# An encoder layer on one core: a ring of its own for weight sums made by DMA, two plain blocks instead of four, the last rows by halves

## The chip, the core and the metric

The kernel runs on one core of one Trainium2 chip, as a single program. The time is the device time of one execution in microseconds (us). Three executions of the kernel before took 1315.06, 1314.51 and 1313.67 us: median 1314.51 us. The engines are TensorE (PE, which also loads weights: PEld), VectorE (DVE), ScalarE (ACT), GpSimd (POOL) and SyncE (SP, which issues most DMAs). Each engine works through its own list of instructions in order and waits on semaphores for the others.

## What is computed

One encoder layer on x of 512 tokens by 1024 features, in float32:

```python
def swiglu(x, w1, w3, w2):
    return (jax.nn.silu(x @ w1) * (x @ w3)) @ w2
...
# x = x + 1/2 * SwiGLU_1(RMSNorm(x))        "ffn a", D_FF = 2816
# x = x + mix(RMSNorm(x))                   two attention branches, gates, w_out
# x = x + 1/2 * SwiGLU_2(RMSNorm(x))        "ffn b"
# output: RMSNorm(x)
```

Each RMSNorm divides by the root of the mean square of a token's 1024 features and multiplies by a gain. The change leaves the attention in the middle alone.

## The kernel before

**Layout.** x lies transposed in eight tiles x[d] of 128 features by 512 tokens. Every product is made of three fp32r matmuls (mm3, lines 195 to 199): each operand is split into a rounded part H and a remainder L, and H*H, H*L and L*H are added. A weight tile of 128x1024 (512 KB) comes by DMA into a raw buffer; ACT casts it to wh (L180) and DVE makes wl (L181) in prep. The raw tiles lie in rings, in which a new tile takes the oldest buffer once its last reader is done: wr (3 buffers), wa (3) and ws (2). The wh/wl pairs have a ring of 3 and one extra buffer, so a wl is made at most some four weight tiles ahead of PE.

**A feed-forward stage.** The 22 blocks of 128 hidden features run in this order: first some plain blocks, by 512-column matmuls (pair, feat; 48 matmuls a block), then groups of pairs of blocks by a Strassen scheme (strassen), each group followed by the eight output rows of w2 that its blocks feed (blocks). GROUPS gives the bounds: in ffn a four plain blocks, then pairs up to 8, 16 and 22, that is groups of 2, 4 and 3 pairs; in ffn b two plain blocks and groups of 3, 4 and 3 pairs. A pair of blocks is seven products, named A11, S1, S2, A12, S3, S4 and A22, each of 24 matmuls of 256 columns: 168 in all, where two plain blocks take 96 matmuls of 512 columns. The pairs are interleaved: pair i has its products at places 7i, 7i+2, ... 7i+12 (slots).

**Weight sums.** A11, A12 and A22 are quarters of the weights as they are. The raws of S1 and S3 are sums: SP loads A21 (L163), and when it has landed POOL issues a DMA that adds A22 or A11 to it in place (L164). S2 and S4 are made by DVE from raws that are there already (L179): S2 = S1 + A11, S4 = S2 + A12. Before the change S1 and S3 lie in wr, beside A22, the plain tiles and the w2 tiles.

**T, statistics and held blocks.** The right operands of S1, S2, S3 and A22 are four sums of quarters of h (TH, TL), made in 16 steps (t_steps, L275 to L283) that the plain part's loop emits between matmuls: hooks["T"] = (first step n, every). The plain part runs before the factors R of the RMSNorm are known: its PSUM banks (the ring "mm" has four) are held, and its evictions (L394, L398, L379) are emitted at the hook stat_R. stat_r (L328, L329, L336) sums the squares on PE, takes ms on DVE and the power on POOL; stat_R (L344, L346) spreads r over the partitions with PE (rb) and copies it to R with ACT. Each hook's n counts the mm3 groups of the plain part.

**The order.** The order on PE is that of the code. The order on ACT, DVE, POOL and SP is set by a list scheduler at build time, from estimated costs. On the chip each engine keeps that order: an instruction that waits holds everything behind it.

**The end.** ffn b's last rows add to x (L443, L444), its squares go to acc, and the last of the eight rows is done in two halves of 256 tokens: after half 0, tail(0) finishes the norm of these tokens and writes them, while PE works on half 1; tail(1) comes after the last matmul (L488 to L518). In tail, POOL does two of the eight multiplications and DVE six (L498).

Of the kernel before, what the change touches and what calls it, by code (L numbers as in the profile page):

```python
# [11 lines left out]
F32 = mybir.dt.float32  # L12
F32R = mybir.dt.float32r
AF = mybir.ActivationFunctionType
# [1 line left out]
PSUM = bass.MemoryType.PSUM  # L16
DRAM = bass.MemoryType.DRAM

BUFS = {"wr": 3, "wa": 3, "ws": 2, "wh": 3, "whx": 1}
GROUPS = {"a": (4, 8, 16, 22), "b": (2, 8, 16, 22)}  # L20
STEPS = ("A11", "S1", "S2", "A12", "S3", "S4", "A22")
GAP_X = 8
GAP_V = 4
# [3 lines left out]
T = 512  # L27
D = 1024
NK = 8
# [11 lines left out]
G_FFN1, G_MIX, G_FFN2, G_FIN, G_BG = 0, 8, 16, 24, 32  # L41
# [14 lines left out]
class Layer:  # L56
# [78 lines left out]
    def load(self):  # L135
        n = len(self.raws)
        if n == len(self.order):
            return False
        name, key = self.order[n][:2]
        tag, last = "wr", n  # L140
        if name[:2] == "sw":
            f, step = key
            tag = {"A11": "wa", "A12": "wa", "S2": "ws", "S4": "ws"}.get(step, "wr")
            last = self.index.get((name, (f, {"A11": "S2", "S1": "S2", "A12": "S4", "S2": "S4"}.get(step))), n)
        raw = self.ring(tag, n, len(self.tiles), last)
        if raw is None:
            return False
        self.raws.append(raw)
        nc = self.nc
        if name[:2] != "sw":  # L150
            nc.sync.dma_start(raw, self.a[name][key])
            return True
        w = self.a["w13" + name[2]]
        dst = raw.rearrange("p (a c) -> p a c", a=2)

        def part(q):
            i, c = 2 * f + int(q[1]) - 1, 512 * (int(q[2]) - 1)
            return w[i:i + 3:2, :, c:c + 512].rearrange("a p c -> p a c")

        if step[0] == "A":  # L160
            nc.sync.dma_start(dst, part(step))
        elif tag == "wr":
            nc.sync.dma_start(dst, part("A21"))  # L163
            nc.gpsimd.dma_start(dst, part("A22" if step == "S1" else "A11"), accum_op=ALU.add)  # L164
        return True
# [148 lines left out]
    def norm_sq(self, d):  # L314
        nc = self.nc
        if d == 0:
            nc.scalar.activation(self.acc, self.x[d], AF.Square)
        else:
            sq = self.tmp.tile([128, T], F32, tag="sq", name="sq", bufs=2)
            nc.scalar.activation(sq, self.x[d], AF.Square)  # L320
            eng = nc.vector if d >= NK - 2 else nc.gpsimd
            eng.tensor_add(self.acc, self.acc, sq)
# [44 lines left out]
    def ffn_run(self, s, gin, gnext, hooks, out, side, gp):  # L367
        nc = self.nc
        g, t, c, half = [], {}, {}, []
# [96 lines left out]
        lo, n = first, 0  # L466
# [15 lines left out]
            g.clear()  # L482
        if out is None:
            return
        self.blocks("w2" + s, rows[:-1], n)
        d, nf = NK - 1, len(g)
        ws = [self.block("w2" + s, n + d * nf + f) for f in range(nf)]
        halves = []  # L488

        def tail(hf):  # L490
            cs = slice(256 * hf, 256 * hf + 256)
            tiles = range(2 * hf, 2 * hf + 2)
            self.stat_r([self.acc[:, :], halves[hf]], tiles)
            yield
            self.stat_R(tiles)
            for e in range(NK):
                y = self.x[e][:, cs]
                (nc.gpsimd if e in (1, 4) else nc.vector).tensor_mul(y, y, self.R[:, cs])  # L498
                (nc.scalar if hf and e % 2 else nc.sync).dma_start(out[e][:, cs], y)
            yield  # L500

        first = None
        for hf in range(2):
            cs = slice(256 * hf, 256 * hf + 256)
            ps = self.bank()
            for f in range(nf):
                self.mm3(ps[:, 0:256], *ws[f], g[f][0][:, cs], g[f][1][:, cs], f == 0, f == nf - 1)
                if hf and f in (nf // 2, nf - 1):
                    next(first)
            xs = self.x[d][:, cs]  # L510
            add(xs, ps[:, 0:256], self.R[:, cs])
            sq = self.tmp.tile([128, 256], F32, tag="sqh", name="sqh", bufs=2)
            nc.scalar.activation(sq, xs, AF.Square)
            nc.scalar.activation(xs, xs, AF.Copy, scale=self.par[:, gnext + d:gnext + d + 1])
            halves.append(sq)
            first = first or tail(0)
        for _ in tail(1):
            pass  # L518

    def bias_open(self, bp):  # L520
# [220 lines left out]
    def rope(self, grp, i, b):  # L741
# [7 lines left out]
        if grp == 0:  # L749
            nc.scalar.activation(self.vH[:, i, :], b[:, 256:512], AF.Copy, scale=rc)  # L750
            nc.vector.scalar_tensor_tensor(self.vL[:, i, :], b[:, 256:512], rc, f32(self.vH)[:, i, :], op0=ALU.mult, op1=ALU.subtract)
        sq = self.tmp.tile([128, T], F32, tag="sq", name="sqb", bufs=2)
        nc.scalar.activation(sq[:, :w], xk[:, :w], AF.Square)
        ss = self.tmp.tile([128, 4], F32, tag="ss", name="ss")
        nc.vector.tensor_reduce(ss[:, :nh], sq[:, :w].rearrange("p (h d) -> p h d", d=128), axis=mybir.AxisListType.X, op=ALU.add)
# [161 lines left out]
    def layer(self, out):  # L917
# [19 lines left out]
                self.norm_sq(d)  # L937

        with tc.tile_pool(name="bt", bufs=1, side="right") as bp:
            hooks = {8: squares, 22: self.stat_r, 26: self.stat_R, "T": (10, 2)}  # L940
            self.bias_open(bp)
            side = {(0, d): lambda g=d: self.bias_rows(g) for d in range(3)}
            for h in range(8):
                side[(0, 4 + h) if h < 4 else (1, h - 4)] = lambda h=h: self.bias_spread(h)
            self.ffn("a", G_FFN1, G_MIX, hooks, side=side)
        self.mixer()
        self.ffn("b", G_FFN2, G_FIN, {7: self.stat_r, 12: self.stat_R, "T": (1, 1)}, out)
        self.hctx.close()


# [92 lines left out]
```

## Time and profile before

| | before |
|---|---|
| median of three executions | 1314.51 us (1313.67 to 1315.06) |
| the profiled execution | 1316.43 us |
| its span (first to last instruction) | 1314.7 us |
| PE busy in the span | 1284.9 us (98%) |
| DVE busy | 832.8 us (63%) |
| ACT busy | 554.4 us (42%) |
| DMA, mean over the span | 124 GB/s |
| stages: plain part of ffn a, last matmul of ffn b | 5.13 to 55.60, 1301.89 us |

A row of a timeline is: start in us from the span's start, duration, engine, line, operation, output <- input, count, and in brackets how long the engine had been idle before it and who released it. A row of a table of windows gives for a stretch its length, the busy time of the engines with the count of instructions, the clock that PE was granted (1.00 is full), the busy share of the DMA engines and GB/s. The profiled execution is 1.7 us longer than its span and 1.9 us above the median.

### The profile page before, as it was taken

The numbers are of one execution on the slowest core, as the hardware profiler recorded it, in microseconds if no ns is written. First come the engines' busy times: TensorE is split into PE (matmuls) and PEld (weight loads), VectorE is DVE, ScalarE is ACT, GpSimd is POOL, SyncE is SP. The second block draws the span as 40 slices with busy tenths as digits, with TensorE's granted clock in tenths as the row PEclk, the third lists the DMA queues.
The fourth block names the chain that finished last, engine by engine and source line by source line (L and its number), as shares of the span: only waits on it lengthen the run. The fifth ranks groups of instructions, "written<-read, shape, count | busy, mean of one in ns | idle before, by whom it ended". The sixth has DMA issues, their size and how long they took to land.

```text
span 1314.7 us, 18852 instructions
## 1 busy us (share of the span) xinstructions
PE 1284.9 (98%) x7580; PEld 1113.4 (85%) x7580; DVE 832.8 (63%) x1227; ACT 554.4 (42%) x829; POOL 120.7 (9%) x106
## 2 busy tenths in 40 slices
PE   7999999999999999999999999999999999999996
PEld 6897999899789877777887778888879989988985
DVE  7775578568632346554575899654487756765774
ACT  7551345145422244144233465543375415432552
POOL 2101100100200000000022300000211010100103
PEclk9999999999999999999999999999999999999998
DMA  7655866544333333232332311345256456645521
GB/s 246 147 172 152 220 162 175 133 124 131 95 96 96 96 87 92 81 82 66 124 98 80 98 63 48 109 157 167 96 128 171 151 128 163 173 130 144 140 86 64
DMA packets 75863, 163.48 MB, mean 124 GB/s; under 512 B 11760, under 2 KB 18304, under 8 KB 75776
## 3 DMA queue, kind: packets, MB, share of 16 engines
q1 hardware_dynamic: 63984, 138.12, 33.4%
q0 software_dynamic: 11072, 23.61, 10.3%
q8 instruction: 59, 0.97, 0.3%
q10 hardware_dynamic: 720, 0.55, 0.1%
q14 instruction: 28, 0.23, 0.1%
HBM read 155.87 MB, written 10.04 MB: 126 GB/s over the span
## 4 chain that ended last, share of the span: by engine, by line
PE 86%; DVE 5%; ACT 3%; issue 2%; DMA 1%; POOL 1%; SPq 0%; DVEq 0%; ACTq 0%; POOLq 0%
PE mm L197 23%; PE mm L199 23%; PE mm L198 23%; PE Y L199 2%; PE Y L198 2%; PE Y L197 2%; ACT P L640 2%; PE S L626 1%; PE X L197 1%; PE X L199 1%; PE X L198 1%; PE Tb L807 1%; PE mm L677 1%; DVE wl L181 1%; DMA wr<-in_w13b 1%
## 5 line engine op out<-in xcount | busy, mean ns | idle before, releaser
L180 ACT CAST wh<-wr 128x1024 fp32r<-128x1024 f32 x195 | 203.8, 1049 | 413.3 <-PE mm L198 287.3
L181 DVE TENSOR_TENSOR wl<-wr,wh 128x1024 fp32r<-128x1024 f32 x195 | 238.3, 1222 | 107.4 <-ACT wh L180 107.0
L197 PE MATMUL mm<-hH,wh 128*128 128x512 f32 (+1 forms) x568 | 212.0, 373 | 5.1 <-ACT wh L931 5.1
L199 PE MATMUL mm<-hH,wl 128*128 128x512 f32 (+1 forms) x568 | 207.6, 365 | 1.2 <-DVE wl L932 0.7
L198 PE MATMUL mm<-hL,wh 128*128 128x512 f32 (+1 forms) x568 | 207.1, 365 | 0.7 <-DVE hL L312 0.6
L198 PE MATMUL mm<-gg,wh 128*128 128x512 f32 (+1 forms) x358 | 139.8, 391 | 1.5 <-DVE gg L389 1.5
L197 PE MATMUL mm<-gg,wh 128*128 128x512 f32 (+1 forms) x358 | 140.2, 392 | 0.2
L199 PE MATMUL mm<-gg,wl 128*128 128x512 f32 (+1 forms) x358 | 139.7, 390 | 0.0
L199 PE MATMUL mm<-TH,wl 128*128 128x256 f32 x456 | 128.1, 281 | 4.0 <-DVE wl L181 4.0
L197 PEld LDWEIGHTS mm<-hH,wh 128*128 128x128 f32 x568 | 107.8, 190 | 25.8 <-ACT wh L931 5.1
L198 PE MATMUL mm<-TL,wh 128*128 128x256 f32 x456 | 127.7, 280 | 0.0
L197 PE MATMUL mm<-TH,wh 128*128 128x256 f32 x456 | 127.7, 280 | 0.0
L199 PEld LDWEIGHTS mm<-hH,wl 128*128 128x128 f32 x568 | 107.4, 189 | 19.9 <-DVE wl L932 1.1
L198 PEld LDWEIGHTS mm<-hL,wh 128*128 128x128 f32 x568 | 107.6, 190 | 17.8 <-DVE hL L312 1.7
L199 PEld LDWEIGHTS mm<-TH,wl 128*128 128x128 f32 x456 | 86.5, 190 | 4.4 <-DVE wl L181 4.4
L197 PEld LDWEIGHTS mm<-TH,wh 128*128 128x128 f32 x456 | 86.5, 190 | 0.0
L198 PEld LDWEIGHTS mm<-TL,wh 128*128 128x128 f32 x456 | 86.4, 189 | 0.0
L198 PEld LDWEIGHTS mm<-gg,wh 128*128 128x128 f32 x358 | 67.4, 188 | 16.9 <-DVE gg L389 2.5
L197 PEld LDWEIGHTS mm<-gg,wh 128*128 128x128 f32 x358 | 67.4, 188 | 16.9 <-ACT gg L388 1.0
L443 DVE TENSOR_TENSOR u<-mm,R 128x512 f32<-128x512 f32 (+1 forms) x49 | 33.3, 679 | 74.1 <-PE mm L199 73.8
L199 PEld LDWEIGHTS mm<-gg,wl 128*128 128x128 f32 x358 | 67.4, 188 | 14.7
L197 PE MATMUL mm<-wh,hH 128*128 128x512 f32 x192 | 77.0, 401 | 0.0
(194 smaller groups left out, 2590.9 us busy)
## 6 DMA issues: line engine op xcount, KB each, us to landing
wr<-in_w13b SPq DMA_DIRECT2D x34, 512.0 KB, 3.7
wr<-in_w13a SPq DMA_DIRECT2D x33, 512.0 KB, 3.8
wr<-in_waq SPq DMA_DIRECT2D x24, 512.0 KB, 3.6
wr<-in_w2a SPq DMA_DIRECT2D x22, 512.0 KB, 3.6
wr<-in_w2b SPq DMA_DIRECT2D x22, 512.0 KB, 3.5
wa<-in_w13b SPq DMA_DIRECT2D x20, 512.0 KB, 3.9
wr<-in_w13b POOLq DMA_DIRECT2D x20, 512.0 KB, 5.8
wa<-in_w13a SPq DMA_DIRECT2D x18, 512.0 KB, 4.1
```

The lines of the kernel that those rows point to most:

```text
L180: self.nc.scalar.copy(H, raw)
L181: self.nc.vector.tensor_sub(L, raw, f32(H))
L197: mm(out, lH, rH, start=start, stop=False, skip_group_check=more)
L198: mm(out, lH, rL, start=False, stop=False, skip_group_check=more)
L199: mm(out, lL, rH, start=False, stop=stop, skip_group_check=more)
L443: nc.vector.tensor_mul(u, ps, R)
L626: nc.tensor.matmul(*args, start=True, stop=True)
L640: nc.scalar.activation(sl, sl, AF.Exp, bias=SO[:, 0, li, h:h + 1], scale=1.0, accum_out=SO[:, 0, li, 2 + h:3 + h])
L677: nc.tensor.matmul(oc, v, p, start=st, stop=sp)
L807: nc.tensor.transpose(pt[:, 128 * j:128 * j + 128], P[h, j][:, 128 * k:128 * k + 128], self.ident)
```

## The change

Five things change. S1 and S3 get a ring of their own, wt, of two buffers, and wa goes from three to two. ffn a has two plain blocks and one more Strassen pair in its first group (3, 4 and 3 pairs, as in ffn b), and its T steps are emitted at every mm3 group from the 10th on instead of at every second one. The squares share the ring "t". In ffn b stat_R stands at the 15th mm3 group of the plain part instead of the 12th. And at the end the last four rows (d = 4 to 7) go by halves: all four rows for tokens 0 to 255, then all four for the rest, with the norm of half 0 spread over the rows of half 1, all its multiplications on DVE, and the sums into acc of these rows on DVE too.

```diff
--- before.py
+++ after.py
@@ -16,8 +16,8 @@
 PSUM = bass.MemoryType.PSUM
 DRAM = bass.MemoryType.DRAM
 
-BUFS = {"wr": 3, "wa": 3, "ws": 2, "wh": 3, "whx": 1}
-GROUPS = {"a": (4, 8, 16, 22), "b": (2, 8, 16, 22)}
+BUFS = {"wr": 3, "wa": 2, "ws": 2, "wt": 2, "wh": 3, "whx": 1}
+GROUPS = {"a": (2, 8, 16, 22), "b": (2, 8, 16, 22)}
 STEPS = ("A11", "S1", "S2", "A12", "S3", "S4", "A22")
 GAP_X = 8
 GAP_V = 4
@@ -140,7 +140,7 @@
         tag, last = "wr", n
         if name[:2] == "sw":
             f, step = key
-            tag = {"A11": "wa", "A12": "wa", "S2": "ws", "S4": "ws"}.get(step, "wr")
+            tag = {"A11": "wa", "A12": "wa", "S2": "ws", "S4": "ws", "S1": "wt", "S3": "wt"}.get(step, "wr")
             last = self.index.get((name, (f, {"A11": "S2", "S1": "S2", "A12": "S4", "S2": "S4"}.get(step))), n)
         raw = self.ring(tag, n, len(self.tiles), last)
         if raw is None:
@@ -159,7 +159,7 @@
 
         if step[0] == "A":
             nc.sync.dma_start(dst, part(step))
-        elif tag == "wr":
+        elif tag == "wt":
             nc.sync.dma_start(dst, part("A21"))
             nc.gpsimd.dma_start(dst, part("A22" if step == "S1" else "A11"), accum_op=ALU.add)
         return True
@@ -316,7 +316,7 @@
         if d == 0:
             nc.scalar.activation(self.acc, self.x[d], AF.Square)
         else:
-            sq = self.tmp.tile([128, T], F32, tag="sq", name="sq", bufs=2)
+            sq = self.tmp.tile([128, T], F32, tag="t", name="sq")
             nc.scalar.activation(sq, self.x[d], AF.Square)
             eng = nc.vector if d >= NK - 2 else nc.gpsimd
             eng.tensor_add(self.acc, self.acc, sq)
@@ -482,39 +482,43 @@
             g.clear()
         if out is None:
             return
-        self.blocks("w2" + s, rows[:-1], n)
-        d, nf = NK - 1, len(g)
-        ws = [self.block("w2" + s, n + d * nf + f) for f in range(nf)]
-        halves = []
-
-        def tail(hf):
+        nf, half = len(g), NK // 2
+        self.blocks("w2" + s, rows[:half], n)
+        ws = [[self.block("w2" + s, n + d * nf + f) for f in range(nf)] for d in range(half, NK)]
+
+        def norm(hf):
             cs = slice(256 * hf, 256 * hf + 256)
             tiles = range(2 * hf, 2 * hf + 2)
-            self.stat_r([self.acc[:, :], halves[hf]], tiles)
+            self.stat_r([self.acc[:, :], sqs[hf]], tiles)
             yield
             self.stat_R(tiles)
             for e in range(NK):
                 y = self.x[e][:, cs]
-                (nc.gpsimd if e in (1, 4) else nc.vector).tensor_mul(y, y, self.R[:, cs])
+                nc.vector.tensor_mul(y, y, self.R[:, cs])
                 (nc.scalar if hf and e % 2 else nc.sync).dma_start(out[e][:, cs], y)
-            yield
-
-        first = None
+                if e % 3 == 2:
+                    yield
+
+        sqs, first = [], iter(())
         for hf in range(2):
             cs = slice(256 * hf, 256 * hf + 256)
-            ps = self.bank()
-            for f in range(nf):
-                self.mm3(ps[:, 0:256], *ws[f], g[f][0][:, cs], g[f][1][:, cs], f == 0, f == nf - 1)
-                if hf and f in (nf // 2, nf - 1):
-                    next(first)
-            xs = self.x[d][:, cs]
-            add(xs, ps[:, 0:256], self.R[:, cs])
-            sq = self.tmp.tile([128, 256], F32, tag="sqh", name="sqh", bufs=2)
-            nc.scalar.activation(sq, xs, AF.Square)
-            nc.scalar.activation(xs, xs, AF.Copy, scale=self.par[:, gnext + d:gnext + d + 1])
-            halves.append(sq)
-            first = first or tail(0)
-        for _ in tail(1):
+            for d in range(half, NK):
+                ps = self.bank()
+                for f in range(nf):
+                    self.mm3(ps[:, 0:256], *ws[d - half][f], g[f][0][:, cs], g[f][1][:, cs], f == 0, f == nf - 1)
+                    if f == nf // 2:
+                        next(first, None)
+                xs = self.x[d][:, cs]
+                add(xs, ps[:, 0:256], self.R[:, cs])
+                sq = self.tmp.tile([128, 256], F32, tag="t", name="sqh")
+                nc.scalar.activation(sq, xs, AF.Square)
+                nc.scalar.activation(xs, xs, AF.Copy, scale=self.par[:, gnext + d:gnext + d + 1])
+                if d < NK - 1:
+                    nc.vector.tensor_add(self.acc[:, cs], self.acc[:, cs], sq)
+                else:
+                    sqs.append(sq)
+            first = norm(hf)
+        for _ in first:
             pass
 
     def bias_open(self, bp):
@@ -749,7 +753,7 @@
         if grp == 0:
             nc.scalar.activation(self.vH[:, i, :], b[:, 256:512], AF.Copy, scale=rc)
             nc.vector.scalar_tensor_tensor(self.vL[:, i, :], b[:, 256:512], rc, f32(self.vH)[:, i, :], op0=ALU.mult, op1=ALU.subtract)
-        sq = self.tmp.tile([128, T], F32, tag="sq", name="sqb", bufs=2)
+        sq = self.tmp.tile([128, T], F32, tag="t", name="sqb")
         nc.scalar.activation(sq[:, :w], xk[:, :w], AF.Square)
         ss = self.tmp.tile([128, 4], F32, tag="ss", name="ss")
         nc.vector.tensor_reduce(ss[:, :nh], sq[:, :w].rearrange("p (h d) -> p h d", d=128), axis=mybir.AxisListType.X, op=ALU.add)
@@ -937,14 +941,14 @@
                 self.norm_sq(d)
 
         with tc.tile_pool(name="bt", bufs=1, side="right") as bp:
-            hooks = {8: squares, 22: self.stat_r, 26: self.stat_R, "T": (10, 2)}
+            hooks = {8: squares, 22: self.stat_r, 26: self.stat_R, "T": (10, 1)}
             self.bias_open(bp)
             side = {(0, d): lambda g=d: self.bias_rows(g) for d in range(3)}
             for h in range(8):
                 side[(0, 4 + h) if h < 4 else (1, h - 4)] = lambda h=h: self.bias_spread(h)
             self.ffn("a", G_FFN1, G_MIX, hooks, side=side)
         self.mixer()
-        self.ffn("b", G_FFN2, G_FIN, {7: self.stat_r, 12: self.stat_R, "T": (1, 1)}, out)
+        self.ffn("b", G_FFN2, G_FIN, {7: self.stat_r, 15: self.stat_R, "T": (1, 1)}, out)
         self.hctx.close()
 
 
```

The lists of DVE show three places. The first is ffn a's start, from the last wl of the plain blocks on (T_264/T_266 and T_265/T_267 are the raw T tiles, t_366 and t_368 the first held block's; L394 is the first eviction of the held banks, L282/L283/L280 are T steps). Before:

```order
L282 TENSOR_TENSOR T_264<-T_264 128x1024
L328 TENSOR_SCALAR ms<-stat 128x4
L181 TENSOR_TENSOR wl<-wr,wh 128x1024
L282 TENSOR_TENSOR T_264<-T_265,T_264 128x1024
L394 TENSOR_TENSOR t_366<-mm,R 128x512
L394 TENSOR_TENSOR t_373<-mm,R 128x512
L283 SCALAR_TENSOR_TENSOR T_265<-T_265,T_264 128x1024
```

After:

```order
L282 TENSOR_TENSOR T_266<-T_266 128x1024
L328 TENSOR_SCALAR ms<-stat 128x4
L181 TENSOR_TENSOR wl<-wa,wh 128x1024
L179 TENSOR_TENSOR ws<-wt,wa 128x1024
L282 TENSOR_TENSOR T_266<-T_267,T_266 128x1024
L280 TENSOR_TENSOR TL<-T_266,TH 128x1024
L283 SCALAR_TENSOR_TENSOR T_267<-T_267,T_266 128x1024
L280 TENSOR_TENSOR TL<-T_266,TH 128x1024
L283 SCALAR_TENSOR_TENSOR T_267<-T_267 128x1024
L181 TENSOR_TENSOR wl<-wt,wh 128x1024
L280 TENSOR_TENSOR TL<-T_267,TH 128x1024 x2
L394 TENSOR_TENSOR t_368<-mm,R 128x512
```

Between the second sum of T and the first eviction now stand six T steps and the wl of S1, and ahead of them the sum for S2, which reads the raw of S1 in wt.

The second place is ffn b's start, after the last of the mixer's squares. Before:

```order
L322 TENSOR_TENSOR acc<-acc,sq 128x512
L179 TENSOR_TENSOR ws<-wr,wa 128x1024
L179 TENSOR_TENSOR ws<-ws,wa 128x1024
L328 TENSOR_SCALAR ms<-stat 128x4
L282 TENSOR_TENSOR T_8344<-T_8344 128x1024
```

After:

```order
L322 TENSOR_TENSOR acc<-acc,sq 128x512
L282 TENSOR_TENSOR T_8432<-T_8432 128x1024
L328 TENSOR_SCALAR ms<-stat 128x4
L181 TENSOR_TENSOR wl<-wr,wh 128x1024
L282 TENSOR_TENSOR T_8432<-T_8433,T_8432 128x1024
```

The two weight sums have left the place ahead of ms: both stand some 25 rows earlier, between the mixer's last weight tiles.

The third place is the end of ffn b's second group (four pairs), where the third pair's A22 is prepared (the wl<-wr here). Before:

```order
L181 TENSOR_TENSOR wl<-ws,wh 128x1024
L415 TENSOR_TENSOR c_9869<-mm,c_9869 128x512
L181 TENSOR_TENSOR wl<-wr,wh 128x1024
L181 TENSOR_TENSOR wl<-wa,wh 128x1024
L417 TENSOR_TENSOR c_9868<-Y,c_9868 128x512
```

After:

```order
L181 TENSOR_TENSOR wl<-ws,wh 128x1024
L415 TENSOR_TENSOR c_9957<-mm,c_9957 128x512
L179 TENSOR_TENSOR ws<-wt,wa 128x1024
L181 TENSOR_TENSOR wl<-wr,wh 128x1024
L181 TENSOR_TENSOR wl<-wa,wh 128x1024
L417 TENSOR_TENSOR c_9956<-Y,c_9956 128x512
```

A sum of the next group (ws<-wt,wa) stands ahead of that wl; ahead of the first two A22 of the group such a sum stands in both lists.

## The prediction

> **What bounds the kernel now.** I read the page's busy times and chain first, then PE's idle brackets in the timeline, then who stood ahead of the late instruction.
>
> ```profile
> span 1314.7 us, 18852 instructions
> PE 1284.9 (98%) x7580; PEld 1113.4 (85%) x7580; DVE 832.8 (63%) x1227; ACT 554.4 (42%) x829; POOL 120.7 (9%) x106
> PE 86%; DVE 5%; ACT 3%; issue 2%; DMA 1%; POOL 1%; SPq 0%; DVEq 0%; ACTq 0%; POOLq 0%
> ```
>
> PE is busy for 98% of the span and holds 86% of the chain that ends last. So only three things can move the time: matmuls that PE no longer runs, stalls of PE, and what PE loses behind a stall. The long stalls in mid-kernel are three: 1.26, 2.40 and 2.72 us. After the last two PE is slow for a while:
>
> ```profile
> 189.10 0.38 PE L199 MATMUL mm<-TH,wl 128*128 128x256 f32 x1 [1.26 <-DVE wl L181]
> 965.42 1.12 PE L344 MATMUL rb<-ident,r 128*128 128x128 f32 x4 [2.40 <-POOL r L329]
> 1129.42 0.58 PE L199 MATMUL mm<-TH,wl 128*128 128x256 f32 x1 [2.72 <-DVE wl L181]
> ...
> 189.10:192.00 2.90, 2.90 (x24) 1.00 0.48 170
> 965.42:968.80 3.38, 3.38 (x11) 0.53 0.98 257
> 1129.42:1132.62 3.20, 3.20 (x15) 0.53 0.64 180
> 1132.62:1136.00 3.38, 3.38 (x32) 1.00 0.79 230
> ```
>
> The lower four rows are windows of PE: length, busy, (matmuls), granted clock, DMA share, GB/s. After 1129.42 the clock is 0.53 for 3.2 us and 15 matmuls start where 30 fit at the next row's pace: 1.6 us lost, so this stall costs 2.7 + 1.6 = 4.3 us. At 965 the 3.38 us hold four short ones (rb) and seven of 512 columns, which at full speed take 0.23 each (96 in 22.00 us, quoted below): some 1.4 us lost, 3.8 in all. After 1.26 us the clock stays at 1.00, and the stall costs little more than its length. I take: a stall of 2.4 us or more costs 1.4 to 1.7 us beyond its length.
>
> The Trainium skill, "TensorE: Matmul & The Clock Gate", HAM oscillation, puts the limit at idle gaps of more than about 3.4 us, and Part 1 calls the window free-running; the stalls of 2.40 and 2.72 us here went cold, so the measurement decides. By the page's limit the loop stalls below would each be 1.6 us cheaper, and the sum some 5 us lower.
>
> **The change part by part.**
>
> *One Strassen pair for two plain blocks.*
>
> ```profile
> 5.13:33.60 28.47, 26.63 (x108) 20.51 (x109) 23.88 (x28) 23.68 (x45) 8.58 (x6) 1.00 0.78 267
> 33.60:55.60 22.00, 22.00 (x98) 18.07 (x97) 18.70 (x20) 12.30 (x16) 3.81 (x3) 1.00 0.60 139
> 55.60:75.40 19.80, 19.80 (x171) 19.76 (x170) 13.53 (x13) 9.84 (x12) 1.20 (x1) 1.00 0.71 178
> ```
>
> The windows are the two plain blocks that stay, the two that go (96 matmuls in 22.00 us) and a stretch as long as a pair (171 in 19.80, so 168 in 19.5 to 19.7). Gain: **-2.3 us**. At the same time 22 us of cover go: these two blocks hid the T steps, the first weight sum and the held evictions.
>
> *ffn a's start.* PE has four "mm" banks, all held by the two plain blocks. The first Strassen product, A11, needs a fifth, so it waits for the first eviction (L394). Before, L394 came right behind the second sum of T:
>
> ```profile
> 18.14 0.80 SPq L151 DMA_DIRECT2D wr<-in_w13a  x2
> 18.99 0.43 SPq L161 DMA_DIRECT2D wa<-in_w13a  x1
> 21.77 1.05 ACT L180 CAST wh<-wr 128x1024 fp32r<-128x1024 f32 x1 [2.13 <-DMA wr<-in_w13a]
> ...
> 25.74 1.22 DVE L282 TENSOR_TENSOR T<-T 128x1024 f32<-128x1024 f32 x1
> 27.15 0.16 DVE L328 TENSOR_SCALAR ms<-stat 128x4 f32<-128x4 f32 x1 [0.18 <-PE stat L336]
> 29.95 1.22 DVE L282 TENSOR_TENSOR T<-T,T 128x1024 f32<-128x1024 f32 x1
> 31.08 1.29 DVE L394 TENSOR_TENSOR t<-mm,R 128x512 f32<-128x512 f32 x2
> ...
> 52.30 1.20 POOL L164 DMA_DIRECT2D wr<-in_w13a  x1 [6.40 <-DVE wl L181]
> 61.54 1.23 DVE L179 TENSOR_TENSOR ws<-wr,wa 128x1024 f32<-128x1024 f32 x1 [2.92 <-issue]
> 954.16 1.24 POOL L164 DMA_DIRECT2D wr<-in_w13b  x1 [8.22 <-DVE x L903]
> 960.79 1.23 DVE L179 TENSOR_TENSOR ws<-wr,wa 128x1024 f32<-128x1024 f32 x1 [4.23 <-DMA wr<-in_w13b]
> DMA to landing us min/median/max: 5.5/5.9/9.2
> ```
>
> Now DVE's list has L179 (the sum for S2) in front, which waits for the accumulating DMA into S1's raw, and then eight operations of 128x1024 before L394. S1's A21 is the third 512-KB load from 18.14 on, issued at about 19.3. The load issued at 18.14 landed at 21.77 (3.6 us); with two others under way I give 5 to 6: 24.3 to 25.3. POOL then issues L164, and its landing, from POOL's start to the waiting DVE, took 6.6 us at 954.16 and 9.2 at 52.30: L = 30.9 at the least and 34.5 at the most; I take 31.5, near the lower row, since the last line gives a median of 5.9. From L on DVE runs nine operations of 1.13 to 1.14 us from start to start (29.95 to 31.08) and a first L394 of 0.6 to 0.7: A11 can begin at L + 10.9 = 42.4, where before the plain part of these two blocks ended at 33.60. Stall 8.8 us, cold 1.7: **+10.5 us**. From above: L = 34.5 gives 11.8 + 1.7 = 13.5. From below: if the sum's DMA were never late, the chain starts when ACT has the raw T tiles, at about 29 (the second L282 starts at 29.95 today); eight operations and L394 give 38.7, a stall of 5.1, with cold 6.8. Below nothing is excluded, since PE has no bank.
>
> *ffn b's start.*
>
> ```profile
> 962.05 1.23 DVE L179 TENSOR_TENSOR ws<-ws,wa 128x1024 f32<-128x1024 f32 x1
> 963.19 0.15 DVE L328 TENSOR_SCALAR ms<-stat 128x4 f32<-128x4 f32 x1
> 963.44 1.93 POOL L329 TENSOR_TENSOR r<-ms,mhalf 128x4 f32<-128x4 f32 x1 [0.24 <-DVE ms L328]
> ```
>
> PE's stall at 965.42 is this chain: ms stood behind two sums, the first of which waited 4.23 us for the same kind of DMA. Now the sums stand earlier, ms can run right after the sum of squares on PE (which ends at about 959.5), r is ready by 962 to 963, and rb is asked for three matmul groups (2.1 us) later than before, at about 965. The stall goes with its cold time: **-3.8 us** (at the least -2.4). Next late could be L394 for A11's bank; it stands behind seven operations here, at 969 to 971, some 3 us before PE is through the plain part.
>
> *The loops in the groups.* S1(k+1)'s raw takes the buffer of S1(k), so its load waits for wl of S1(k), and the sum that reads it (L179) stands on DVE ahead of wl for A22(k-1), which PE needs before it frees a buffer for wl of S1(k+1). One turn, by ffn b's second group:
>
> ```profile
> 1104.60 1.23 DVE L179 TENSOR_TENSOR ws<-wr,wa 128x1024 f32<-128x1024 f32 x1 [4.60 <-DMA wr<-in_w13b]
> 1114.25 1.21 DVE L181 TENSOR_TENSOR wl<-wr,wh 128x1024 fp32r<-128x1024 f32 x1
> 1120.37 1.21 POOL L164 DMA_DIRECT2D wr<-in_w13b  x1 [0.64 <-DMA wr<-in_w13b]
> 1127.01 1.23 DVE L179 TENSOR_TENSOR ws<-wr,wa 128x1024 f32<-128x1024 f32 x1 [5.54 <-issue]
> 1128.15 1.22 DVE L181 TENSOR_TENSOR wl<-wr,wh 128x1024 fp32r<-128x1024 f32 x1
> ```
>
> From sum to sum 22.4 us, while PE needs 19.7 us a pair: each turn eats 2.7 us of margin, and the second turn in each four-pair group is the stall (189.10, 1129.42). The own ring keeps this: with two buffers for S1 and S3 in turn, S1(k+1) still gets S1(k)'s. What changes is the group's ends. Before, the next group's S1(0) lay in wr behind the w2 tiles; now it takes the next wt buffer, and the scheduler puts its sum ahead of an A22 too. So there is one more turn in each first and second group: four in all. Each costs between 0 (margin left) and 2.7 + 1.6 = 4.3 us. In ffn a's group 1 the first turn eats the margin and the second leaves a stall of about 2; in its group 2 a third turn follows one that already stalls: 2.7, mostly cold, 3.5; ffn b's group 1 (two turns now) 3; in ffn b's group 2 the cold time gives 1.6 us of margin back, 1.1. Sum **+9.6 us**, from 0 to 17.
>
> The Trainium skill, "DMA: Bandwidth & Descriptors", Anatomy of one DMA, fits a POOL-issued DMA as 2.0 us plus bytes over 436e3, which is 3.2 us for 512 KB (an estimate from that page); the trace's 5.5 to 9.2 us decide. By the page a turn would take 19.7 us, no turn would stall, and A11 would start 3.4 us earlier: the sum would be about 13 us lower.
>
> *The end.*
>
> ```profile
> 1301.92 0.42 DVE L443 TENSOR_TENSOR u<-mm,R 128x256 f32<-128x256 f32 x1 [0.66 <-PE mm L199]
> 1302.99 3.16 DVE L498 TENSOR_TENSOR x<-x,R 128x256 f32<-128x256 f32 x6 [0.18 <-ACT R L346]
> 1306.07 0.15 DVE L328 TENSOR_SCALAR ms<-stat 128x2 f32<-128x2 f32 x1
> 1307.05 0.69 PE L344 MATMUL rb<-ident,r 128*128 128x128 f32 x2 [2.71 <-POOL r L329]
> 1308.18 3.16 DVE L498 TENSOR_TENSOR x<-x,R 128x256 f32<-128x256 f32 x6 [1.96 <-ACT R L346]
> ```
>
> ms of half 1 stood behind half 0's six multiplications (3.16 us). Now those are done earlier, so ms can start when PE's stat is in, about 1.7 us earlier; against it go two more multiplications on DVE (2 x 0.53), and some 0.2 us of extra evictions: **-0.5 us**, from -1.5 to +1.
>
> The later statistic on its own, the shared ring for squares and two wa buffers cost nothing I can see: the wa loads land 5 us or more before their casts.
>
> **Sum**: -2.3 + 10.5 - 3.8 + 9.6 - 0.5 = +13.5 us. The profiled execution took 1316.43 us, 1.9 above the median of the runs; against its own time I get 1329.9, and as a median of runs **1328 us**.
>
> **The rivals.**
>
> *A: faster.* The own ring takes the stalls of the loops away instead of adding turns. Before, wr was shared by S1, S3, A22 and, at the group's ends, w2 tiles; if a turn was long because S1's load stood behind these on SP's queue, an own ring shortens it below 19.7 us. For it: SP keeps one list, and A21 is issued 0.9 us and more after the wl it waits for. Against it: of the 22.4 us, 6.6 are the accumulating DMA and 9.65 (1104.60 to 1114.25) PE's own pace, and the ring changes neither. It decides if a turn falls by 2.7 us. Then -1.4 and -4.3 for the old stalls, the start at its lower bound +6.8, and -2.3 - 3.8 - 0.5: -5.5, **1309 us**.
>
> *B: only the start counts.* PE is so late after the start, and the margins so large, that the extra turns hide: 13.5 - 9.6 = +3.9, **1318 us**.
>
> *C: dearer turns.* Every extra turn stalls and goes cold (17) and the start's DMA is slow (13.5): -2.3 - 3.8 - 0.5 + 17 + 13.5 = +23.9, **1338 us**.
>
> *D: no visible change*, the gains, a start at its lower bound and no extra stall: -2.3 + 6.8 - 3.8 - 0.5 = +0.2, **1314.5 us**.
>
> **How the numbers follow.** The forecast 0.45, A 0.17, B 0.18, C 0.12, D 0.08. A measurement of this kernel can tell 0.2% (2.6 us) from no change. Slower by more: forecast, B and C, 0.75; within: D, 0.08; faster: A, 0.17. The range 8 times in 10 leaves out half of A and half of C: 1309 to 1338; the forecast's own is 1321 to 1334.
>
> **What would show it.** Right: a PE bracket of 7 to 12 us at about 33.6, released by DVE's L394, with a clock near 0.5 behind it, and DVE idle before L179 until the DMA into wt; no bracket before rb in ffn b; in groups 1 and 2 one bracket of 1 to 3 us more, released by wl (L181), with L179 idle ahead of it. Wrong: A11 starting before 38; groups without such brackets (A or B); a turn from L179 to L179 below 20 us (A).

## The result: 3.3% slower, where 1.0% was forecast

The changed kernel took **1357.95 us** (median; 1356.58 to 1360.74) beside 1314.51 us for the kernel before: ratio 1.0334, 95% interval 1.0316 to 1.0352. The forecast was 1328 us with a range to 1338: the sign was right, the size was three times too small. The two profiled executions, 1356.58 and 1316.43 us, differ by 40.2 us where the medians differ by 43.4.

The page of the changed kernel:

```profile
span 1354.1 us, 19105 instructions
PE 1297.0 (96%) x7706; PEld 1129.0 (83%) x7706; DVE 842.1 (62%) x1248; ACT 559.2 (41%) x839; POOL 115.6 (9%) x102
PE 72%; DVE 10%; DMA 8%; issue 6%; ACT 4%; POOL 1%; POOLq 0%; DVEq 0%; SPq 0%; ACTq 0%
```

PE holds 72% of the chain that ends last, where it held 86%; DVE went from 5% to 10% and DMA from 1% to 8%. PE's waits of the changed kernel, in total, times, longest:

```profile
PE mm L199 <- DVE wl L181: 17.2, 10, 3.2
PE mm L197 <- DVE t L394: 11.8, 1, 11.8
PE mm L197 <- DVE c L415: 6.9, 4, 2.1
```

The first of these was 4.5 us in three waits before, the other two did not exist. Stage by stage, PE's windows (length, busy, matmuls, clock, DMA share, GB/s) give the ledger. Before: plain part of ffn a, its groups 1 and 2, the mixer with ffn b's plain part, ffn b's groups 1 and 2, the end:

```profile
5.00:55.68 50.68, 48.72 (x204) 1.00 0.70 211
55.68:95.20 39.52, 39.52 (x338) 1.00 0.62 169
...
141.97:222.81 80.84, 79.58 (x674) 1.00 0.67 182
...
326.88:980.43 653.55, 646.31 (x3230) 1.00 0.32 97
980.43:1037.79 57.36, 57.36 (x506) 1.00 0.63 173
...
1082.26:1163.40 81.14, 78.42 (x674) 0.98 0.62 163
...
1265.46:1314.70 49.24, 37.61 (x184) 0.88 0.16 54
```

The same stages of the changed kernel:

```profile
5.00:45.36 40.36, 27.27 (x109) 0.90 0.75 235
45.36:112.51 67.15, 63.74 (x504) 0.93 0.66 161
...
159.94:248.34 88.40, 81.40 (x674) 0.98 0.64 156
...
353.37:1002.72 649.35, 644.50 (x3231) 1.00 0.32 99
1002.72:1071.14 68.42, 62.36 (x505) 0.95 0.64 155
...
1115.86:1205.60 89.74, 82.61 (x674) 0.94 0.64 161
...
1307.35:1354.10 46.75, 37.19 (x238) 0.94 0.17 57
```

The start: 22.0 us of plain blocks are gone, but the plain part is only 10.3 shorter, so 11.7 us of stall. Group 1 of ffn a grew by 27.6, of which 19.7 are the third pair: 7.9 lost, about 2.8 of them the cold clock behind the start's stall (26 matmuls in the 5.64 us from 45.36 on, at a granted clock of 0.50). The mixer and ffn b's plain part: -4.2. The other groups 1 and 2: +7.6, +11.1 and +8.6. The end: -2.5. The w2 rows between groups add 1.9 and the third groups take off 0.4. Together 39.4 us, the difference of the spans (1354.1 and 1314.7 us).

The forecast's start, in DVE's timeline of the changed kernel:

```profile
34.30 1.23 DVE L179 TENSOR_TENSOR ws<-wt,wa 128x1024 f32<-128x1024 f32 x1 [6.18 <-DMA wt<-in_w13a]
...
44.53 1.28 DVE L394 TENSOR_TENSOR t<-mm,R 128x512 f32<-128x512 f32 x2
```

The sum waited for the accumulating DMA until 34.30, near the upper bound of the forecast (34.5), and L394 followed 10.2 us later, as summed. PE's bracket at 45.36 is 11.81 us.

One of the four lossy groups, ffn b's second, with DVE's sums and PE's brackets:

```profile
1139.94 1.23 DVE L179 TENSOR_TENSOR ws<-wt,wa 128x1024 f32<-128x1024 f32 x1 [6.67 <-DMA wt<-in_w13b]
1162.59 1.22 DVE L179 TENSOR_TENSOR ws<-wt,wa 128x1024 f32<-128x1024 f32 x1 [5.78 <-issue]
1185.42 1.23 DVE L179 TENSOR_TENSOR ws<-wt,wa 128x1024 f32<-128x1024 f32 x1 [5.86 <-DMA wt<-in_w13b]
...
1142.36 0.38 PE L199 MATMUL mm<-TH,wl 128*128 128x256 f32 x1 [1.43 <-DVE wl L181]
1165.00 0.58 PE L199 MATMUL mm<-TH,wl 128*128 128x256 f32 x1 [3.22 <-DVE wl L181]
1187.84 0.39 PE L199 MATMUL mm<-TH,wl 128*128 128x256 f32 x1 [0.41 <-DVE wl L181]
1201.16 0.43 PE L197 MATMUL mm<-TH,wh 128*128 128x256 f32 x1 [2.07 <-DVE c L415]
```

A turn takes 22.65 and 22.83 us, the 22.4 of the forecast. But the first turn stalls too (1142.36, the first A22), and behind the last turn PE waits for an eviction (L415) that stands in DVE's list behind the late work. Before, this group had one bracket. The third sum is the next group's, which did not stand in this group before.

### The profile page after: what moved, and what is told of

Same layout as the page of the kernel before. It is cut to its first block, busy times and chain, and to the rows that moved or that the text cites. A ratio compares the mean times of both kernels' runs of the same rounds, so it can differ in the third digit from the quotient of the medians.

```text
span 1354.1 us, 19105 instructions
## 1 busy us (share of the span) xinstructions
PE 1297.0 (96%) x7706; PEld 1129.0 (83%) x7706; DVE 842.1 (62%) x1248; ACT 559.2 (41%) x839; POOL 115.6 (9%) x102
## 3 DMA queue, kind: packets, MB, share of 16 engines
q0 software_dynamic: 11616, 24.66, 10.3%
## 4 chain that ended last, share of the span: by engine, by line
PE 72%; DVE 10%; DMA 8%; issue 6%; ACT 4%; POOL 1%; POOLq 0%; DVEq 0%; SPq 0%; ACTq 0%
PE mm L197 20%; PE mm L199 20%; PE mm L198 20%; DVE wl L181 4%; DMA wt<-in_w13b 3%; DMA wt<-in_w13a 3%; ACT P L644 2%; PE S L630 1%; PE Y L197 1%; PE Y L199 1%; PE Y L198 1%; PE Tb L811 1%; PE mm L681 1%; DMA wr<-in_w2a 1%; PE X L197 1%
## 5 line engine op out<-in xcount | busy, mean ns | idle before, releaser
L180 ACT CAST wh<-wr 128x1024 fp32r<-128x1024 f32 x154 | 161.1, 1049 | 355.5 <-PE mm L198 241.9
L181 DVE TENSOR_TENSOR wl<-wr,wh 128x1024 fp32r<-128x1024 f32 x154 | 189.0, 1228 | 85.7 <-ACT wh L180 83.2
L197 PE MATMUL mm<-hH,wh 128*128 128x512 f32 (+1 forms) x544 | 202.4, 372 | 16.8 <-DVE t L394 11.8
L199 PE MATMUL mm<-hH,wl 128*128 128x512 f32 (+1 forms) x544 | 198.1, 364 | 0.6 <-DVE wl L181 0.5
L198 PE MATMUL mm<-hL,wh 128*128 128x512 f32 (+1 forms) x544 | 197.4, 363 | 0.6 <-DVE hL L312 0.6
L199 PE MATMUL mm<-TH,wl 128*128 128x256 f32 x480 | 139.6, 291 | 16.7 <-DVE wl L181 16.7
L197 PE MATMUL mm<-TH,wh 128*128 128x256 f32 x480 | 138.7, 289 | 6.9 <-DVE c L415 6.9
L198 PE MATMUL mm<-TL,wh 128*128 128x256 f32 x480 | 138.3, 288 | 0.0
L199 PEld LDWEIGHTS mm<-TH,wl 128*128 128x128 f32 x480 | 95.1, 198 | 18.5 <-DVE wl L181 18.5
L179 DVE TENSOR_TENSOR ws<-wt,wa 128x1024 f32<-128x1024 f32 x20 | 24.5, 1225 | 103.8 <-issue 48.6
L443 DVE TENSOR_TENSOR u<-mm,R 128x512 f32<-128x512 f32 (+1 forms) x52 | 33.7, 649 | 88.3 <-PE mm L199 88.2
```

Source lines behind the costliest of these rows:

```text
L179: self.nc.vector.tensor_add(raw, a, b)
L180: self.nc.scalar.copy(H, raw)
L181: self.nc.vector.tensor_sub(L, raw, f32(H))
L197: mm(out, lH, rH, start=start, stop=False, skip_group_check=more)
L198: mm(out, lH, rL, start=False, stop=False, skip_group_check=more)
L199: mm(out, lL, rH, start=False, stop=stop, skip_group_check=more)
```

## The experiments

Each is compared with runs of the kernel before on the same chip (medians 1314.5 to 1316.0 us); the ratio is given with its 95% interval. The experiments ran on three chips, so a difference in us between two of them can be off by up to 1.5 us for that reason alone.

**e1: four plain blocks again, own ring kept**

```diff
-GROUPS = {"a": (2, 8, 16, 22), "b": (2, 8, 16, 22)}
+GROUPS = {"a": (4, 8, 16, 22), "b": (2, 8, 16, 22)}
-            hooks = {8: squares, 22: self.stat_r, 26: self.stat_R, "T": (10, 1)}
+            hooks = {8: squares, 22: self.stat_r, 26: self.stat_R, "T": (10, 2)}
```

> The change with ffn a's four plain blocks and its T steps left as before (own ring wt, later statistic, last rows by halves kept). Theory 'two separate losses' (11.8 us of start behind the missing bank plus 2.4 us of cold clock; turns of the weight sums in the groups, about 30 us): the start's bracket behind DVE L394 goes, the brackets released by wl (L181) and by L415 stay in ffn a's four-pair group and in ffn b's groups 1 and 2: 1338 to 1345 us. Rival 'late start' (PE reaches the first group 11.8 us late with all engines out of step, and the brackets of the groups follow from it): the brackets go in ffn a and the time falls to 1310 to 1325 us.

Measured 1344.71 us, 1.0220 (1.0197 to 1.0243). PE's waits:

```profile
PE mm L199 <- DVE wl L181: 18.9, 9, 3.5
PE mm L197 <- DVE c L415: 6.7, 4, 2.2
```

The wait for L394 is gone, and the brackets of the groups are all there: they do not follow from the late start. The two plain blocks fewer, with their T steps, cost 13 us of the 43 (15 by the ratios).

**e2: S1 and S3 in wr again, all else of the change kept**

```diff
-BUFS = {"wr": 3, "wa": 2, "ws": 2, "wt": 2, "wh": 3, "whx": 1}
+BUFS = {"wr": 3, "wa": 3, "ws": 2, "wh": 3, "whx": 1}
-            tag = {"A11": "wa", "A12": "wa", "S2": "ws", "S4": "ws", "S1": "wt", "S3": "wt"}.get(step, "wr")
+            tag = {"A11": "wa", "A12": "wa", "S2": "ws", "S4": "ws"}.get(step, "wr")
-        elif tag == "wt":
+        elif tag == "wr":
```

> The change with S1 and S3 back in wr (wa 3 buffers, no wt), all else kept. Theory 'two separate losses': the start's bracket of 10 to 13 us behind DVE L394 stays, the groups lose only the two brackets of before (at the second A22 of the four-pair groups): 1314.5 - 2.3 + 14.2 - 3 (statistic) - 2.5 (last rows) = 1321 us, 1317 to 1325. Rival 'late start': brackets in the groups as in the change, 1345 us or more.

Measured 1324.57 us, 1.0065 (1.0040 to 1.0090). PE's waits:

```profile
PE mm L197 <- DVE t L394: 10.9, 1, 10.9
PE mm L199 <- DVE wl L181: 6.3, 3, 4.7
```

The start stays and the groups keep the two brackets of before, the second of them longer (4.74 us, where it was 2.72). So the own ring costs the larger part: 33 us between this run and the change (35 by the ratios). The two causes are separate, as in the theory. This run also takes wa back to three buffers; e6 keeps two and loses nothing by it.

**e3: neither; only the statistic and the halves.** Its edits are those of e1 and e2 together.

> The kernel before with only the later statistic of ffn b, the shared ring for the squares and the last four rows by halves. Theory: the statistic saves 3 to 3.8 us although ms still stands behind the two weight sums, since rb is asked for three matmul groups later; the last rows save 2.5 us (their part of the change's trace): 1308 to 1310 us. Rival: the statistic's gain came from the sums' new place on DVE alone, so that a bracket of 1.5 us or more stays before rb: 1311 to 1313 us.

Measured 1312.19 us, 0.9967 (0.9950 to 0.9984): the rival's number, 3.8 us below the kernel before on its chip, but for another reason than the rival's. The bracket before rb is gone, as the theory had it, and the end is 2.3 us shorter. But the bracket at ffn b's second A22 grew from 2.72 to 4.58 us. POOL and DVE there:

```profile
1117.49 2.50 POOL L164 DMA_DIRECT2D wr<-in_w13b  x2 [21.35 <-DMA wr<-in_w13b]
...
1126.10 1.23 DVE L179 TENSOR_TENSOR ws<-wr,wa 128x1024 f32<-128x1024 f32 x1 [7.51 <-issue]
...
1110.88 2.10 SPq L163 DMA_DIRECT2D wr<-in_w13b  x2
```

A21 was issued at 1110.88 and POOL could start at 1117.49, 6.6 us later (4.8 before); both accumulating DMAs then went out together. Why these A21 loads came later was not settled.

**e4: one ring of four buffers for S1, S3 and A22** (e3 with)

```diff
-BUFS = {"wr": 3, "wa": 3, "ws": 2, "wh": 3, "whx": 1}
+BUFS = {"wr": 4, "wa": 3, "ws": 2, "wh": 3, "whx": 1}
```

> As the run before it (later statistic, halves), with S1, S3 and A22 in one ring of four buffers (wr 4, wa 3), which is as much memory as the change's wr 3, wt 2, wa 2. Theory 'turn': a turn is long because S1(k+1) gets the buffer of S1(k), three tiles back; with four buffers it gets that of S3(k-1), so the load starts some 5 us earlier, and the brackets at the second A22 of the four-pair groups (1.26 and 2.72 us with their cold clock, 5.7 us in all) go: 5 us below the run before it, 1302 to 1305 us. Rival 'the DMA itself': the accumulating DMA sets the pace however early its buffer is free: no change, 1308 to 1310 us.

Measured **1308.47 us, 0.9947 (0.9929 to 0.9964)**, 3.7 us below e3 and the fastest of this study. That misses the theory's 1302 to 1305 and lies in the rival's 1308 to 1310, but the rival had the brackets stay, and they did not: those at the second A22 shrank to 0.57 and 0.51 us. The sums in ffn b's second group:

```profile
1099.11 1.22 DVE L179 TENSOR_TENSOR ws<-wr,wa 128x1024 f32<-128x1024 f32 x1 [2.74 <-DMA wr<-in_w13b]
...
1121.78 1.23 DVE L179 TENSOR_TENSOR ws<-wr,wa 128x1024 f32<-128x1024 f32 x1 [5.82 <-issue]
```

They come 2.6 and 4.3 us earlier than e3's (1101.71 and 1126.10), with the group beginning at the same time to within 0.4 us. The turn between them, 22.7 us, is 1.7 us shorter than e3's but no shorter than the 22.4 of the kernel before; the larger part of the gain is the earlier start, enough for both turns. With the same memory as the change's three rings it is some 49 us faster than the change.

**e5: no accumulating DMA**

```diff
-            nc.gpsimd.dma_start(dst, part("A22" if step == "S1" else "A11"), accum_op=ALU.add)
+            pass
```

> The change without POOL's accumulating DMA (L164): S1 and S3 are then A21 alone, so the sums' second addend is left out of the computation; rings, order of the stages and DVE's additions stay. Theory 'the wait for the accumulating DMA': with it go 6 us and more of each turn (22.4 us to about 16, below PE's 19.1 to 19.7 a pair), all brackets of the groups go, and the start keeps only the nine operations of DVE ahead of L394 (A11 at 38 to 40 instead of 45.4): 1310 to 1317 us. Rival 'the ring and DVE's own work': brackets in the groups stay at half or more of their 27 us: 1330 us or more.

S1 and S3 are A21 alone here: the kernel leaves out the second addend, and with the wait for this DMA its traffic too. Measured 1310.26 us, 0.9961 (0.9946 to 0.9977). No bracket above 0.3 us is left in any group. The one at the start is 5.6 us, with A11 at 39.74:

```profile
PE mm L197 <- DVE t L394: 5.6, 1, 5.6
```

With the ring, the stages and DVE's additions as in the change, this DMA, by its wait or its traffic, is necessary for all of the groups' loss and for about half of the start's. The other half goes with the nine operations of DVE ahead of L394. The forecast's lower bound for this case was 38.7.

**e6: own ring, but S1 of each group's first pair in wr** (e1 with)

```diff
-            tag = {"A11": "wa", "A12": "wa", "S2": "ws", "S4": "ws", "S1": "wt", "S3": "wt"}.get(step, "wr")
+            tag = {"A11": "wa", "A12": "wa", "S2": "ws", "S4": "ws", "S1": "wr" if f in GROUPS[name[2]] else "wt", "S3": "wt"}.get(step, "wr")
-        elif tag == "wt":
+        elif step in ("S1", "S3"):
```

> The run with four plain blocks and the own ring (e1, 1344.7 us), but S1 of each group's first pair is loaded into wr again, as before; the other S1 and all S3 stay in wt. Theory 'preload': what costs is not the own ring but that with S1 of the first pair in wt, S1 of the second pair finds no buffer ahead of the group and the next group's first sum comes early, ahead of an A22; put back, the brackets at the first and last A22 of each group and those released by L415 go, only the second A22 of the four-pair groups stays: 1310 to 1316 us. Rival 'two buffers are too few': S3 and S1 in turn in two buffers still wait, 1325 us or more.

Measured 1311.17 us, 0.9981 (0.9968 to 0.9994), 33.5 us below e1 (31 by the ratios). PE's waits:

```profile
PE mm L199 <- DVE wl L181: 5.6, 4, 2.8
```

All L415 brackets and all but one of the new ones are gone; that one is 1.11 us, at ffn b's first A22. The own ring of two is harmless within a group. The loss comes from the one tile per group that it took from wr: with it in wt, S1 of the second pair is loaded later (for ffn b's second group SP issued its A21 16.3 us ahead of the group before, 8.3 in the change), and the next group's first sum stands ahead of an A22. Which of these two costs how much was not separated. Both occur in e1: ffn b's first group stalls 2.44 us at its first A22 already, while in its second group the first A22 has no bracket, the second 2.89 us, much as before, and the third, behind the next group's sum, 2.94 us.

**e7: ring of four, two plain blocks, T steps from the fourth matmul group on** (e4 with)

```diff
-GROUPS = {"a": (4, 8, 16, 22), "b": (2, 8, 16, 22)}
+GROUPS = {"a": (2, 8, 16, 22), "b": (2, 8, 16, 22)}
-            hooks = {8: squares, 22: self.stat_r, 26: self.stat_R, "T": (10, 2)}
+            hooks = {8: squares, 22: self.stat_r, 26: self.stat_R, "T": (4, 1)}
```

> The ring of four (e4, 1308.5 us) with two plain blocks as in the change, and ffn a's T steps from the fourth matmul group on: in DVE's list L394 then stands behind the wl that waits for the accumulating DMA and one T step, instead of nine operations. Theory 'queue on DVE': A11 starts some 2.5 to 3 us after that DMA has landed, at 36 to 39 instead of 45.4; stall 3 to 5 us with cold clock 1.5, less 2.3 for the matmuls: 1310 to 1314 us. Rival 'the bank': A11 waits for the first eviction whatever stands ahead, stall of 8 us or more: 1316 to 1320 us.

Measured 1317.72 us, 1.0022 (1.0004 to 1.0041), in runs from 1312.94 to 1321.53: 4 us above the expected range and inside the rival's. The rival's bracket of 8 us is not there, though: A11's is 2.34 us, and A11 starts at 39.32, partly since the early T steps brought a new wait: PE's sum of squares stood 2.98 us behind DVE's acc.

```profile
24.75 1.49 DVE L322 TENSOR_TENSOR acc<-acc,sq 128x512 f32<-128x512 f32 x2 [3.90 <-POOL acc L322]
...
38.49 1.28 DVE L394 TENSOR_TENSOR t<-mm,R 128x512 f32<-128x512 f32 x2
```

L394 comes 6 us earlier than in the change, which is the queue theory's part. At the end of ffn a's first group this run is 4.4 us behind e4 (100.18 and 95.80), within what was expected. The rest of the 9 us lost against e4 lies where nothing was edited: the mixer and ffn b's plain part took 654.91 us (650.81 in e4) and ffn b's second group 80.23 us (77.60 in e4). Why is open.

**e8: a bank of the other ring for A11 of ffn a's first pair**

```diff
-                st[f, bank] = self.bank() if bank == "A" else self.aux(bank)
+                st[f, bank] = self.bank() if bank == "A" and not (s == "a" and f == 2) else self.aux(bank)
```

> The change with a PSUM bank of the other ring (aux) for A11, S2, S3 and A22 of ffn a's first pair, so that A11 needs no eviction. Theory 'the bank, then S1': A11 starts at 33.6, and S1 waits instead for its wl and T, which stand in the same list on DVE and come at about 42.5: the bracket moves behind A11 and shrinks from 11.8 to about 6 us: 1350 to 1353 us. Rival 'bank only': no bracket of more than 2 us, 1343 to 1346 us.

Measured 1357.81 us, 1.0329 (1.0313 to 1.0344): nothing gained. PE's brackets at the start:

```profile
37.59 0.38 PE L197 MATMUL Y<-TH,wh 128*128 128x256 f32 x1 [0.43 <-ACT wh L180]
39.98 0.58 PE L198 MATMUL Y<-TL,wh 128*128 128x256 f32 x1 [2.01 <-DVE TL L280]
44.52 0.58 PE L199 MATMUL Y<-TH,wl 128*128 128x256 f32 x1 [3.96 <-DVE wl L181]
54.95 0.39 PE L199 MATMUL X<-hH,wl 128*128 128x256 f32 x1 [2.15 <-DVE wl L181]
```

A11 ran at 34.17 and the wait moved to S1's T and wl and on to A12, 8.6 us in four brackets; the group's second A22 then waited 4.88 us (1.34 in the change), and the group ended at 113.59 (112.51 in the change). The bank is where the wait shows; DVE's list is what PE waits for. The expected 5 us fell with that.

**e9: the later statistic alone, on the kernel before**

```diff
-        self.ffn("b", G_FFN2, G_FIN, {7: self.stat_r, 12: self.stat_R, "T": (1, 1)}, out)
+        self.ffn("b", G_FFN2, G_FIN, {7: self.stat_r, 15: self.stat_R, "T": (1, 1)}, out)
```

> The kernel before with one number changed: ffn b's stat_R at the 15th matmul group instead of the 12th. Theory: the bracket of 2.40 us before rb and its cold clock go (4.1 us in e3's trace), but PE then reaches the four-pair group of ffn b earlier and meets the same turn there: up to 2.4 us come back at the second A22 (4.58 us of bracket in e3 against 2.72): 1311 to 1314 us. Rival: the wider bracket in e3 belongs to the shared ring of squares and the halves: the whole 4.1 us stays, 1310 to 1311 us beside 1314.5.

Measured 1314.78 us, 0.9997 (0.9986 to 1.0009): no change, a little above the theory's range. In the trace PE enters ffn b's first group 4.4 us earlier, and the bracket at the second A22 of its second group is 4.04 us instead of 2.72, which makes that group 2.4 us longer (83.56 us against 81.14). So the wider bracket does not belong to the halves. With stat_R at 15 and S1 and S3 in a wr of three, it is 4.0 to 4.7 us in three traces (e2, e3, e9); with stat_R at 12 it is 2.7 and 2.8 us (before, e10). PE's earlier arrival does not explain it: the sum ahead of the first A22 stands 22.2 us behind the group's start, as before (22.3). It is the next turn that took 23.9 us instead of 22.4; POOL could start its DMA 6.4 us after A21 was issued, where it was 4.8 before. Why is not shown.

**e10: the last four rows by halves alone**, with the shared ring of squares: e3 with stat_R at 12.

> The kernel before with only the last four rows by halves and the shared ring for the squares. Theory: 2.4 us at the end (46.9 us from the last Strassen product to the end in e3, 49.2 before), nothing elsewhere: 1311.5 to 1313 us beside 1314.5. Rival: half-wide rows cost as much as the shorter end saves once the rest is as before: 1314 to 1315 us.

Measured 1313.45 us, 0.9986 (0.9974 to 0.9997), half a microsecond above the expected range and 1.8 us below the kernel before on its chip, where 2.4 was forecast for the end; the trace's end is 2.2 us shorter. The end, ms to the multiplications:

```profile
1303.44 0.16 DVE L328 TENSOR_SCALAR ms<-stat 128x2 f32<-128x2 f32 x1 [1.15 <-PE stat L336]
...
1305.31 2.77 DVE L497 TENSOR_TENSOR x<-x,R 128x256 f32<-128x256 f32 x8 [1.71 <-ACT R L346]
```

## Why the prediction was right and wrong, step by step

**The pair for two plain blocks.** -2.3 us was not disturbed by anything seen: with the start's loss and the brackets set apart, ffn a's first group is as long as three pairs (63.74 us busy less 2.8 and 1.7 of cold clock is 59.2; three times 19.7 is 59.1).

**ffn a's start.** The mechanism was right link by link: sum, nine operations, L394, bracket. The size was 11.7 + 2.8 = 14.5 against +10.5; the term mis-sized is the landing of the accumulating DMA, 9.1 us from POOL's start (25.22) to the sum (34.30), where I took a value near 6.6. The kernel before has three such DMAs between 36 and 53 us, which took 5.8, 5.9 and 9.2 us to land, so the rows left either value open, and the range that I gave covered it. And the part read as the cause of the wait, the missing bank, is only its place (e8).

**ffn b's start.** -3.8 forecast, -4.2 found (-4.1 in e9 for the same stretch), and in the change r is ready at 987.2 and rb starts at 991.3. That the sums ahead of ms would have to move was not needed: in e9, where they stay, the bracket goes too.

**The groups.** This is the step that failed: "one more turn in each first and second group: four in all", +9.6 us with 17 as its bound. The runs showed 34.3 (5.1, 7.6, 11.1 and 8.6 in the groups, 1.9 in the w2 rows behind them). The length of a turn was right (22.65 to 22.83). Wrong was what a turn starts from. I had written that the own ring "keeps this" and counted only the added turn at a group's end; but in the ring of two the first pair's S1 and S3 fill both buffers, so S1 of the second pair, which had a third buffer in wr, comes later. The sums for the second and the third pair of ffn b's first group, before and in the change:

```profile
983.23 1.22 DVE L179 TENSOR_TENSOR ws<-wr,wa 128x1024 f32<-128x1024 f32 x1
1001.30 1.23 DVE L179 TENSOR_TENSOR ws<-wr,wa 128x1024 f32<-128x1024 f32 x1 [3.43 <-DMA wr<-in_w13b]
...
1012.03 1.23 DVE L179 TENSOR_TENSOR ws<-wt,wa 128x1024 f32<-128x1024 f32 x1 [4.05 <-DMA wt<-in_w13b]
1028.45 1.22 DVE L179 TENSOR_TENSOR ws<-wt,wa 128x1024 f32<-128x1024 f32 x1 [7.88 <-DMA wt<-in_w13b]
```

The group starts at 980.43 and 1002.72. So they stood 2.8 and 20.9 us behind its start and now stand 9.3 and 25.7 us behind it, and PE's first bracket there is 2.53 us (1030.87). In the four-pair groups the delay of the third pair's sum is smaller, 2.2 us in ffn a and 1.7 in ffn b. So nine A22 of these groups stall, where two did, not one more per group. The L415 brackets, 6.9 us and their cold clock, were in no sum. e6 undoes this one assignment and the 33.5 us come back; e5 shows that without the accumulating DMA no turn stalls at all. How the 34.3 us divide between the later start and the added turn is open.

**The end.** -0.5 forecast, -2.5 found. From the last u (L443) to ms it is now 2.03 us (1344.26 to 1346.29) where it was 4.15, so the term for ms was -2.1 instead of -1.7. The surcharge for two more multiplications on DVE was wrong in sign: eight take 2.77 us there (e10's row), where six beside POOL's two took 3.16.

**The rivals.** C, dearer turns, was the nearest, with the right places; even it stopped at a bound of 17 us, since each turn was priced and the number of turns that stall was not doubted. B and D fall with the brackets in the groups. A is refuted for this ring: no turn fell by 2.7 us. A ring of four, shared, does take most of the old stalls away (e4), though its turn stays at 22.7 us. And A's argument that SP issues A21 0.9 us and more after the wl that it waits for does not come out of the trace: the wl at 1112.50 ends at 1113.73, and A21 is issued at 1113.76.

**The clock rule.** The Trainium skill, "TensorE: Matmul & The Clock Gate", HAM oscillation, warns of idle gaps of more than some 3.4 us; by that limit the changed kernel's stalls of 2.07 to 3.22 us would have left the clock alone. They show both answers (last section), so the measurement decides, and the sum by the page would have been further off. **The DMA rule.** The estimate of 3.2 us for a 512-KB transfer from POOL, worked out from the Trainium skill, "DMA: Bandwidth & Descriptors", Anatomy of one DMA, does not hold for the accumulating form here: 5.6 to 10.0, median 5.9.

```profile
DMA to landing us min/median/max: 5.6/5.9/10.0
```

## What to carry to other kernels

Giving a tile class its own ring takes it out of a ring that was also its prefetch depth: count how many tiles of the class are in flight *ahead* of each stage before and after, not only how many buffers a steady turn uses. When a loop through a DMA is longer than the engine's work per turn, the loss depends on the head start (e4), and a gain elsewhere can be partly lost at the next such loop (e9, for a reason that is open). And a wait that shows at a bank or an eviction is worth following to the list of the engine that should free it, because giving the bank moves the wait and saves nothing (e8).

## What the runs showed of the hardware

The clock after a stall does not go by the stall's length alone. PE's windows of the changed kernel right behind a stall of 2.75 us and one of 2.07 us:

```profile
209.45:212.35 2.90, 2.90 (x24) 1.00 0.54 194
108.10:111.40 3.30, 3.30 (x19) 0.64 1.08 256
```

The longer one kept the full clock, the shorter did not. The trace shows what differs. The stretches at half clock last 3.41 us or a multiple of it (the last one runs into the kernel's end), and they start on one grid: behind the stalls of mid-kernel at 109.03, 231.91, 1030.63, 1068.18, 1163.75 and 1201.30, all whole multiples of 3.413 us apart. Cut along this grid, the stall of 2.75 us falls into two windows and that of 2.07 us into one:

```profile
204.61:208.02 3.41, 2.09 (x18) 1.00 0.56 102
208.02:211.43 3.41, 1.98 (x16) 1.00 0.21 71
211.43:214.84 3.41, 3.41 (x32) 1.00 0.76 252
...
105.62:109.03 3.41, 1.34 (x12) 1.00 1.00 202
109.03:112.44 3.41, 3.41 (x19) 0.50 1.07 317
```

PE was idle for 1.32 and 1.43 us of the first two windows, and the clock stayed. It was idle for 2.07 us of the fourth, and the fifth ran at 0.50. Once the first matmul had run, each full-clock window of the changed kernel with 1.97 us of idle time or more was followed by a window at half clock, and none with 1.44 or less was. Between the two the runs give no sharp limit: 1.70 us were followed by half clock in e7 (960.89 to 964.30, longest stall 1.33 us), 1.83 us were not in e1 (232.63 to 236.05). This grid agrees with the free-running window of the Trainium skill, "TensorE: Matmul & The Clock Gate", Part 1. For a sum it means that a stall of 2 to 3 us costs its length plus 0 to 1.7 us, by where it falls. Behind the stall of 3.22 us, of which 1.25 us fell into the next window, the half clock lasted for two windows (1163.75 to 1170.58).

And DVE's half-wide multiplications at the end took 0.35 us each (eight in 2.77 us) where POOL did none, and 0.53 us each (six in 3.16 us) where POOL did two of its own at the same time (from 1308.22, 1.83 us).
